# The last store of an attention-score kernel, issued as three transfers

## The chip, the cores and the metric

The kernel runs on one core of one Trainium2 chip. The metric is the device time of one execution in microseconds (us), on that one core. Beside it there is a profile of one execution, whose span runs from its first to its last instruction and is a little shorter than the time.

## The reference

For 64 heads (batch 8, heads 8) of 512 positions and 64 features, all products of a query with a key, scaled:

```python
def setup_inputs():
    batch, heads, seq, dim = 8, 8, 512, 64
    return {"q": np.random.randn(batch, heads, seq, dim).astype(np.float32),
            "k": np.random.randn(batch, heads, seq, dim).astype(np.float32)}

def reference(q, k):
    scale = 1.0 / np.sqrt(q.shape[-1])
    return (np.einsum('bhqd,bhkd->bhqk', q, k) * scale).astype(np.float32)
```

The inputs are 16.8 MB together and the output is 67.1 MB in float32, so most of what the core moves is output.

## The kernel before

The work is cut into 16 tiles (`CHUNKS * UNITS`, four each), numbered by `g`. One tile is the scores of four heads: 128 partitions x 2 x 4096 float32, 4 MB. Here `P` is 128, `RO` is 8 and `S` is 512. A partition of a tile holds two runs (`x`) of `RO * S` = 4096 numbers, 16 KB each, and each run is contiguous in the output as well. Three buffers in SBUF, `bigs`, take turns; the loaded inputs pass through them too.

```python
    store_sems = [nc.alloc_semaphore(f"store{n}") for n in range(3)]
    ...
    out_r = out.rearrange("(v b) (t x h) (u i) k -> (v b t) (h u) x (i k)", b=2, x=2, h=2, i=RO)

    bigs = [nc.alloc_sbuf_tensor(f"big{n}", [P, 2, RO, S], f32)[:] for n in range(3)]
    ...
    def store_buffer(g):
        return bigs[(0, 2, 1)[g % 3]]
```

The inputs are loaded, cast to bfloat16 by GpSimd, transposed and multiplied by TensorE. ScalarE and VectorE move the products from PSUM to the tile's buffer, 128 x 1024 numbers at a time, and scale them on the way:

```python
        for g in range(CHUNKS * UNITS):
            o = store_buffer(g)
            for p in range(parity, PAIRS, 2):
                ...
                scaled(o[:, x, i:i + 2, :], pss[p % 3]).then_inc(
                    sem[f"free{p % 3}"] if p < PAIRS - 2 else drained, 1)
```

(`drained` is `out_act` for ScalarE and `out_dve` for VectorE.) SyncE issues one store for each tile once both engines have finished it, and at the end waits for all stores. The increment of `next` lets TensorE go on to a further tile:

```python
    for g in range(CHUNKS * UNITS):
        nc.sync.wait_ge(sem["out_act"], g + 1)
        nc.sync.wait_ge(sem["out_dve"], g + 1).then_inc(sem["next"], 1)
        nc.sync.dma_start(out=out_r[g], in_=store_buffer(g).rearrange("p x i k -> p x (i k)")
                          ).then_inc(store_sems[g % 3], 16)
    for n in range(3):
        nc.sync.wait_ge(store_sems[n], 16 * len(range(n, 4 * UNITS, 3)))
```

A store counts as done when its semaphore has gone up by 16; in the trace these arrive as 16 single landings[...]. GpSimd waits for the store two tiles back before it lets a buffer be filled again:

```python
    for g in range(2, CHUNKS * UNITS - 1):
        ...
        nc.gpsimd.wait_ge(store_sems[(g - 2) % 3], 16 * ((g - 2) // 3 + 1)
                          ).then_inc(sem["room"], 1)
```

Of the kernel before, what the change touches and what calls it, by code (L numbers as in the profile page):

```python
# [5 lines left out]
def kernel(  # L6
# [5 lines left out]
    nc = tc.nc  # L12
    B, H, S, D = q.shape
    scale = 1.0 / (D ** 0.5)
    P = 128
    UNITS = B // 2
# [4 lines left out]
    RO = 8  # L21
# [6 lines left out]
    CHUNKS = 4  # L28
# [10 lines left out]
    sem = {name: nc.alloc_semaphore(name) for name in names}  # L39
    load_sems = [nc.alloc_semaphore(f"load{n}") for n in range(2 * UNITS)]  # L40
    store_sems = [nc.alloc_semaphore(f"store{n}") for n in range(3)]

    q_r = q.rearrange("(v b) g (m j) d -> v (b g m) (j d)", b=2, j=R)
    k_r = k.rearrange("(v b) g (m j) d -> v (b g m) (j d)", b=2, j=R)
    out_r = out.rearrange("(v b) (t x h) (u i) k -> (v b t) (h u) x (i k)", b=2, x=2, h=2, i=RO)
# [26 lines left out]
    def xf(v):  # L72
        return bigs[(0, 1, 2, 1)[v]].rearrange("p x i k -> p (x i k)").rearrange(
            "p (x s c) -> p x s c", x=2, s=2)

    def store_buffer(g):
        return bigs[(0, 2, 1)[g % 3]]

    def load(v, x):
        nc.sync.dma_start(out=xf(v)[:, x],  # L80
                          in_=(k_r, q_r)[x][v].rearrange("p (s c) -> p s c", s=2)
                          ).then_inc(load_sems[2 * v + x], 16)
# [9 lines left out]
    for x in range(2):  # L92
        nc.sync.wait_ge(sem["cast"], x + 1)
        load(UNITS - 1, x)
    for g in range(CHUNKS * UNITS):
        nc.sync.wait_ge(sem["out_act"], g + 1)
        nc.sync.wait_ge(sem["out_dve"], g + 1).then_inc(sem["next"], 1)
        nc.sync.dma_start(out=out_r[g], in_=store_buffer(g).rearrange("p x i k -> p x (i k)")
                          ).then_inc(store_sems[g % 3], 16)
    for n in range(3):  # L100
        nc.sync.wait_ge(store_sems[n], 16 * len(range(n, 4 * UNITS, 3)))


    nc.gpsimd.memset(identity, 0.0).then_inc(sem["ident"], 1)
# [10 lines left out]
    def cast(v, x, s, j0, j1, dst):  # L115
        src = xf(v)[:, x, s]
        if x == 0:
            src = src.rearrange("p (j e d) -> p j e d", e=2, d=D)[:, j0:j1]
            dst = dst[:, :, s].rearrange("p j d e -> p j e d")
        else:  # L120
            src = src.rearrange("p (j e i d) -> p j e i d", e=2, i=RO, d=D)
            dst = dst[:, :, s].rearrange("p (i j) d e -> p j e i d", i=RO)
        return nc.gpsimd.tensor_copy(out=dst, in_=src)  # L123

    for v in range(UNITS):
        for x in range(2):
# [4 lines left out]
            if v == 1 and x == 0:  # L131
# [3 lines left out]
                last = cast(v, x, 1, 0, W, xs)  # L135
                last.then_inc(sem["ready"], 1)
            else:
                for s in range(2):
                    last = cast(v, x, s, 0, JP, xb[:, w0:w0 + JP])
# [140 lines left out]
```

## Time and profile before

| what | value |
|---|---|
| time, median of 3 executions (lowest to highest) | 203.05 us (202.89 to 203.07) |
| span of the profiled execution | 201.3 us |
| TensorE busy | 100.6 us, 50% |
| VectorE busy | 106.2 us, 53% |
| ScalarE busy | 86.8 us, 43% |
| GpSimd busy | 58.4 us, 29% |
| moved by DMA | 83.91 MB, mean 417 GB/s |
| read from and written to HBM | 16.78 MB and 67.11 MB |
| stores | 16, of 4096 KB each, median 19.7 us from issue to landing |
| loads | 8, of 2048 KB each, median 15.3 us (k) and 17.8 us (q) |

How to read it: the busy times say how long each engine worked and not whether it set the pace. The time from issue to landing of a transfer includes its wait behind those issued earlier. The page also has a row that gives the mean busy share of the core's 16 DMA engines in 40 slices of the span, in tenths, and under it the rate in GB/s. For finer questions the trace can be asked for any stretch of the span: busy time of each engine, share and rate of the DMA engines there (a packet counts for the stretch in which it starts).

### The profile page before, as it was taken

What the parts mean: (1) busy time and instruction counts of PE and PEld (TensorE: products, weight loads), DVE (VectorE), ACT (ScalarE), POOL (GpSimd) and SP (SyncE); (2) the same over time, 40 slices, a digit from 0 to 9 for tenths busy, and PEclk for the clock granted to TensorE, in tenths of its full rate; (3) what the DMA queues carried; (4) which work ended last, traced back from release to release, by engine and by line L of the source; (5) the groups of instructions that cost most, each with busy time, mean ns of one, the idle gap of its engine ahead of it and who ended that gap; (6) DMA issues with size and microseconds to landing.
All of it is one profiled execution on the core that took longest, in us unless ns stands there. A gap on an engine that the chain in (4) does not pass through costs nothing. (4 is left out here: it accounts for less than half of the span.)

```text
span 201.3 us, 1617 instructions
## 1 busy us (share of the span) xinstructions
PE 100.6 (50%) x368; PEld 50.0 (25%) x384; DVE 106.2 (53%) x98; ACT 86.8 (43%) x98; POOL 58.4 (29%) x34
## 2 busy tenths in 40 slices
PE   0037492375667637566665775477536464730000
PEld 0036350141334314232431333143202121200000
DVE  0665556076847696575769375927653636350000
ACT  0204576264645657374656355635434444440000
POOL 0399999999303030303030303030000000000000
PEclk9999969579957999888899589957996969696555
DMA  6999999999999999999999999999999999999993
GB/s 202 423 420 446 433 423 430 433 413 433 420 426 446 423 426 436 433 423 426 446 423 430 436 433 420 430 443 423 430 430 439 423 423 433 433 425 423 426 436 150
DMA packets 5507, 83.91 MB, mean 417 GB/s; under 512 B 384, under 2 KB 384, under 8 KB 384
## 3 DMA queue, kind: packets, MB, share of 16 engines
q1 hardware_dynamic: 5504, 83.89, 98.1%
q14 instruction: 3, 0.02, 0.0%
HBM read 16.78 MB, written 67.11 MB: 417 GB/s over the span
## 5 line engine op out<-in xcount | busy, mean ns | idle before, releaser
L173 PE MATMUL ps<-kT,qz 128*128 x240 | 79.7, 452 | 61.7 <-PEq L162 60.1
L247 DVE TENSOR_SCALAR big<-ps 128x1024 f32<-128x1024 f32 x64 | 77.0, 1222 | 51.5 <-PE ps L173 51.1
L244 ACT ACTIVATE big<-ps 128x1024 f32<-128x1024 f32 x64 | 64.9, 1023 | 69.4 <-PE ps L173 66.8
L173 PEld LDWEIGHTS ps<-kT,qz 128*128 x256 | 27.7, 108 | 106.8 <-issue 100.9
L112 POOL COPY xs<-xb 128x2048 bf16<-128x2048 bf16 x10 | 18.9, 1893 | 67.2 <-DMA out_dram<-big 67.0
L123 POOL CAST xb<-big 128x2048 bf16<-128x2048 f32 (+1 forms) x16 | 36.3, 2321 | 3.5 <-DMA big<-in_k_dram 2.8
L158 PE MATMUL tp<-identity,xs 128*128 128x128 f32 x96 | 17.8, 347 | 1.1 <-PEq L162 1.1
L158 PEld LDWEIGHTS tp<-identity,xs 128*128 128x128 f32 x96 | 16.1, 187 | 5.8 <-issue 5.2
L216 DVE COPY kT<-tp 64x512 f32<-64x512 f32 x14 | 9.7, 694 | 6.3 <-PE tp L158 5.8
L216 ACT COPY kT<-tp 64x512 f32<-64x512 f32 x14 | 8.1, 577 | 11.4 <-PE tp L158 11.2
L216 DVE COPY qz<-tp 64x512 f32<-64x512 f32 x12 | 8.3, 694 | 6.3 <-PE tp L158 6.1
L221 DVE MEMSET qz<- 128x4096 uint32 x2 | 6.9, 3472 | 6.8 <-PEq L89 6.0
L216 ACT COPY qz<-tp 64x512 f32<-64x512 f32 x12 | 7.5, 621 | 3.0 <-PE tp L158 2.8
L158 PE MATMUL tp<-identity,xb 128*128 128x128 f32 x8 | 1.9, 424 | 13.5 <-PEq L162 13.5
L158 PE MATMUL ps<-identity,xb 128*128 128x128 f32 x24 | 5.6, 422 | 1.3 <-PEq L162 1.3
L158 PEld LDWEIGHTS ps<-identity,xb 128*128 128x128 f32 x24 | 5.0, 228 | 1.6 <-issue 1.6
L158 PEld LDWEIGHTS tp<-identity,xb 128*128 128x128 f32 x8 | 1.6, 223 | 13.5 <-issue 13.5
L216 DVE COPY qz<-ps 64x512 f32<-64x512 f32 x4 | 2.8, 694 | 2.1 <-PE ps L158 2.1
L216 ACT COPY qz<-ps 64x512 f32<-64x512 f32 x4 | 2.6, 641 | 2.5 <-PE ps L158 2.4
L216 ACT ACT_TABLE_LOAD x1 | 1.3, 1283 | 5.0 <-PEq L89 5.0
L123 POOL CAST xs<-big 128x1024 bf16<-128x1024 f32 x2 | 2.7, 1337 | 0.2 <-DMA big<-in_k_dram 0.2
L112 ACT COPY xs<-xb 128x2048 bf16<-128x2048 bf16 x1 | 1.9, 1891 | 0.0
(8 smaller groups left out, 3.4 us busy)
## 6 DMA issues: line engine op xcount, KB each, us to landing
out_dram<-big SPq DMA_DIRECT2D x16, 4096.0 KB, 19.7
big<-in_k_dram SPq DMA_DIRECT2D x4, 2048.0 KB, 15.3
big<-in_q_dram SPq DMA_DIRECT2D x4, 2048.0 KB, 17.8
```

Source lines behind the costliest of these rows:

```text
L112: copy(out=xs.rearrange("p w s d e -> p (w s d e)"), in_=xb[:, w0:w0 + W].rearrange("p w s d e -> p (w s d e)")).then_inc(sem["ready"], 1)
L123: return nc.gpsimd.tensor_copy(out=dst, in_=src)
L158: ins = pe.transpose(out=dst[:, w], identity=identity, in_=src[:, w])
L173: ins = pe.matmul(out=ps[:, w, :], lhsT=qz[:, bass.ds(n2 + x, 1), i + w].rearrange("p n c -> p (n c)"), rhs=keys[:, bass.ds(n2 + x, 1)].re ...
L216: copy(out=dst, in_=src[:, h]).then_inc(sem["moved"], 1)
L221: engine.memset(qz[:, v * N:(v + 1) * N], 0.0).then_inc(sem["zeroed"], 1)
L244: lambda o, ps: nc.scalar.mul(out=o, in_=ps, mul=scale),
L247: lambda o, ps: nc.vector.tensor_scalar(out=o, in0=ps, scalar1=scale, scalar2=None, op0=mult),
```

## The change

The stores of the first 15 tiles stay. The last tile's store becomes three transfers, each with a semaphore of its own. `edge` is 3072 numbers, so the first transfer takes the first 12 KB of each run of all 128 partitions. The second takes the remaining 4 KB of each run of partitions 0 to 119, and the third the same of partitions 120 to 127. By the change's description the first runs over 16 DMA engines, the second over 15 and the third over 8. It is for the end of the kernel: it deals the last tile's bytes unequally over the DMA engines, with fewer of them for one engine.

```diff
+    part_sems = [nc.alloc_semaphore(f"part{n}") for n in range(3)]
 ...
+    edge = 3 * RO * S // 4
+    parts = [(slice(0, P), slice(0, edge)), (slice(0, P - 8), slice(edge, RO * S)),
+             (slice(P - 8, P), slice(edge, RO * S))]
+    last = CHUNKS * UNITS - 1
     for g in range(CHUNKS * UNITS):
         nc.sync.wait_ge(sem["out_act"], g + 1)
         nc.sync.wait_ge(sem["out_dve"], g + 1).then_inc(sem["next"], 1)
-        nc.sync.dma_start(out=out_r[g], in_=store_buffer(g).rearrange("p x i k -> p x (i k)")
-                          ).then_inc(store_sems[g % 3], 16)
+        src = store_buffer(g).rearrange("p x i k -> p x (i k)")
+        if g < last:
+            nc.sync.dma_start(out=out_r[g], in_=src).then_inc(store_sems[g % 3], 16)
+        else:
+            for n, (rows, cols) in enumerate(parts):
+                nc.sync.dma_start(out=out_r[g][rows, :, cols], in_=src[rows, :, cols]
+                                  ).then_inc(part_sems[n], 16)
     for n in range(3):
-        nc.sync.wait_ge(store_sems[n], 16 * len(range(n, 4 * UNITS, 3)))
+        nc.sync.wait_ge(store_sems[n], 16 * len(range(n, last, 3)))
+    for n in range(3):
+        nc.sync.wait_ge(part_sems[n], 16)
```

## The prediction, made before the changed kernel ran

> **What bounds the kernel now.** I read the page's second and third parts first. The span is 201.3 us, and in all but its first and last slices the DMA engines are at nine tenths:
>
> ```profile
> DMA  6999999999999999999999999999999999999993
> GB/s 202 423 420 446 433 423 430 433 413 433 420 426 446 423 426 436 433 423 426 446 423 430 436 433 420 430 443 423 430 430 439 423 423 433 433 425 423 426 436 150
> ...
> q1 hardware_dynamic: 5504, 83.89, 98.1%
> ```
>
> One queue on 16 engines moves 83.89 MB and is busy for 98.1% of the span, so the kernel is bound by its transfers and no arithmetic matters. The reader is to see the exception: the last slice, digit 3 at 150 GB/s. Then the waits of the queue that issues the transfers, and the end of its timeline:
>
> ```profile
> SPq L97 <- DVE big L247: 143.5, 16, 13.6
> SPq L101 <- DMA out_dram<-big: 21.4, 2, 19.4
> ```
>
> ```profile
> 179.51 0.37 SPq L98 DMA_DIRECT2D out_dram<-big  x1
> ```
>
> The last of the 16 stores is issued at 179.51 and the rest of the span is its landing: 201.3 - 179.5 = 21.8 us. A store of 4 MB at 430 GB/s is 9.75 us; the other 12 us are the store ahead of it in the queue and the drain. Nothing computes after VectorE's eviction at 178.19, so the end is set by DMA alone. I cut the last 5 us into stretches of 0.6 us (columns: stretch, length, the engines' busy times with counts, granted clock, mean busy share of the 16 DMA engines, GB/s):
>
> ```profile
> 197.00:197.60 0.60, 0.00 (x0) 0.00 (x0) 0.00 (x0) 0.00 (x0) 0.00 (x0) 0.50 1.03 437
> 197.60:198.20 0.60, 0.00 (x0) 0.00 (x0) 0.00 (x0) 0.00 (x0) 0.00 (x0) 0.50 0.39 164
> 198.20:198.80 0.60, 0.00 (x0) 0.00 (x0) 0.00 (x0) 0.00 (x0) 0.00 (x0) 0.50 0.07 27
> 198.80:199.40 0.60, 0.00 (x0) 0.00 (x0) 0.00 (x0) 0.00 (x0) 0.00 (x0) 0.50 0.06 27
> 199.40:200.00 0.60, 0.00 (x0) 0.00 (x0) 0.00 (x0) 0.00 (x0) 0.00 (x0) 0.50 0.06 27
> 200.00:200.60 0.60, 0.00 (x0) 0.00 (x0) 0.00 (x0) 0.00 (x0) 0.00 (x0) 0.50 0.06 27
> 200.60:201.30 0.70, 0.00 (x0) 0.00 (x0) 0.00 (x0) 0.00 (x0) 0.00 (x0) 0.50 0.00 0
> ```
>
> This is the finding. A share of 0.06 is one engine of 16 (1/16 = 0.0625); 27 GB/s for 0.6 us is 16 KB, one packet, which is one run of the store. From 198.2 on four such packets start one after the other on a single engine while fifteen have nothing left: 4 x 16 KB = 64 KB in 2.4 us. The trace's record of single landings says the same: of the last store's 16 landings, 14 fall within 0.5 us, the fifteenth 0.3 us later, and the sixteenth 2.16 us after that, at the span's end. The lag is no accident of the last store: with tiles numbered from 0, the last landing is behind the fifteenth by 0.5 us for store 0, 0.2 for store 3, 1.0 for store 6, 1.7 for store 9, and 2.1 to 2.3 for stores 11 to 15. One engine is slower and never catches up, because each store gives each engine 256 KB.
>
> [...] The trace shows one slow engine (and a fifteenth landing 0.3 us late), but not its number.[...]
>
> **The change part by part.** All of it is in the last store's 4 MB; 15 stores, loads and compute stay. The instruction order differs only in the issuing queue: 15 whole stores and three partial ones.
>
> *Removed.* [...] It keeps 8 partitions x 2 runs x 12 KB = 192 KB of 256 KB, so 64 KB fewer: 4 packets of 0.607 us (start to start) = 2.43 us. If it is the slow one, its last data moves from 200.86 (last packet's end) to 198.43.
>
> *Added to others.* The second transfer is 120 x 2 x 4 KB = 960 KB over 15 engines: 64 KB each, as before. The third is 8 x 2 x 4 KB = 64 KB over 8 engines: 8 KB each[...], at 27 GB/s 0.30 us. They were done between 198.0 and 198.7, so they would be done between 198.3 and 199.0.
>
> *Smaller packets and more transfers.* An engine that had 16 packets of 16 KB has 16 of 12 KB and 16 of 4 KB, and two more semaphore writes. The semaphore packets take 9 ns each in the trace. Packets of 4 KB don't occur in it; I allow 0.1 us in all, a guess.
>
> *Issue.* Two more issues of 0.37 us, at about 179.9 and 180.3; the queue still has the store before to move until about 188, so they are hidden. Three more waits at the end have a length of tens of ns (17 ns for the shorter of the two recorded on that line); after landing nothing else is added.
>
> Sum where everything goes as meant: the end of data goes from 200.86 to the later of 198.5[...] and 198.7 to 199.1 (the rest), so 1.8 to 2.2 us less: about 201.1 us of 203.05.
>
> [...]
>
> **The rivals.**
> 1. *The second transfer collides on ports.* [...] 960 KB at about 217 GB/s is 4.8 us instead of 2.4. [...] Against: the change's cut of 64 KB fits the lag closely, as if sized by someone who saw it work.
> 2. *The slow engine isn't the one relieved.* [...] nothing is saved (203.1 to 203.3); [...] it gets 8 KB more, and 203.4 to 204.2. For it: the trace doesn't number engines. [...]
> 3. *The lag belongs to the profiled execution.* In the last 20 us, with compute over, the lag stays at 2.1 to 2.2 us and doesn't grow: all packets then take about 611 ns, while the slow ones before had 634 to 644. So the slow engine is disturbed by something that goes with compute, and that might be the recording itself. Then only the cost of the pieces stays: 203.1 to 204.2. Against: the executions that were timed take 203.05 us, no less than the profiled one's 202.65, where a missing 2 us of tail should show.
> 4. *The pieces land one row after the other in a worse order*[...]. I give it little.
>
> **Range and chances.** As meant without port trouble, 201.1 us: 0.30. With the third transfer slowed, 201.5 to 202.1: 0.25. Rival 1, near 203.9: 0.19. Rivals 2 and 3, 203.1 to 204.2: 0.22. Rival 4: 0.04. The middle of this lies near 202; I put the one figure at 201.8 us, between the two good cases and the rest, and the range from 200.8 to 204.1. The gain can't pass the whole lone tail, 2.4 us or 1.2%, so faster by over 2% (below 199.0) is next to impossible: 0.01. Slower by over 2% needs 4 us (rival 4 or two rivals at once): 0.04. The rest, 0.95, is within 2%.
>
> **What would show it.** Right: in stretches of 0.6 us at the end, the share falls from 1.0 to 0 within about 1.5 us and no run of lines with 0.06 and 27 GB/s is left. [...] Rival 1: for 4 to 5 us before the end a rate near 217 GB/s with the share still near 1, since packets of 4 KB would take about 300 ns instead of about 155. Rival 2: the same 2.4 us of single packets at the end as before. Rival 3: the profiled tail shrinks but the timed executions don't. Wrong altogether: a time below 200.8 us, which would mean that more than the tail had moved, or one above 204.1 us.

## The result, and the profile after

| | before | changed |
|---|---|---|
| time, median (lowest to highest) | 203.05 us (202.89 to 203.07) | 203.34 us (203.22 to 203.65) |
| ratio of the times, 95% interval | 1 | 1.0019 (1.0001 to 1.0036) |
| the same in a later measurement, with 15 executions of the changed kernel | 1 | 1.0021 (1.0013 to 1.0029) |
| span of the profiled execution | 201.3 us | 202.0 us |

The change made the kernel slower by some 0.4 us, where 1.25 us faster was predicted. The page of the changed kernel shows no difference but in the last slices:

```profile
DMA  6999999999999999999999999999999999999995
GB/s 198 428 435 432 425 438 422 428 393 438 425 428 441 425 425 441 422 425 451 422 422 448 422 425 441 425 428 425 444 428 422 444 425 422 441 423 428 419 378 163
...
q1 hardware_dynamic: 5783, 83.89, 98.4%
```

The bytes are the same 83.89 MB. The last slice rose from 3 to 5 tenths busy, but at nearly the same rate, 163 GB/s instead of 150, and the slice before it fell to 378: the engines are busy for longer over the same bytes. The issuing queue's waits, and the instructions that wrote the output (least, median and greatest ns of one, first and last start in us):

```profile
SPq L104 <- DVE big L261: 143.9, 16, 12.9
SPq L115 <- DMA out_dram<-big: 18.6, 3, 16.0
```

```profile
L107 SPq DMA_DIRECT2D out_dram<-big x15: 372/372/402, 34.7 to 169.7; - x15
L110 SPq DMA_DIRECT2D out_dram<-big x3: 372/1277/1404, 180.1 to 182.0; - x3
```

The waits for computing are what they were. In order of time the three issues took 0.37 us (16 engines), 1.40 us (15) and 1.28 us (8), where 0.37 us each was expected, but all three were issued by 183.3, long before an engine needed them. So the loss is in the drain. The end of the span in stretches of 0.6 us (last two columns: mean busy share of the 16 DMA engines, GB/s):

```profile
195.50:196.10 0.60, 0.00 (x0) 0.00 (x0) 0.00 (x0) 0.00 (x0) 0.00 (x0) 0.50 0.75 273
196.10:196.70 0.60, 0.00 (x0) 0.00 (x0) 0.00 (x0) 0.00 (x0) 0.00 (x0) 0.50 1.05 246
196.70:197.30 0.60, 0.00 (x0) 0.00 (x0) 0.00 (x0) 0.00 (x0) 0.00 (x0) 0.50 0.90 205
197.30:197.90 0.60, 0.00 (x0) 0.00 (x0) 0.00 (x0) 0.00 (x0) 0.00 (x0) 0.50 0.83 205
197.90:198.50 0.60, 0.00 (x0) 0.00 (x0) 0.00 (x0) 0.00 (x0) 0.00 (x0) 0.50 0.87 300
...
200.30:200.90 0.60, 0.00 (x0) 0.00 (x0) 0.00 (x0) 0.00 (x0) 0.00 (x0) 0.50 0.14 55
200.90:201.50 0.60, 0.00 (x0) 0.00 (x0) 0.00 (x0) 0.00 (x0) 0.00 (x0) 0.50 0.07 27
```

Two things stand here. From 196 to 198 the share is near 1 and the rate is 205 to 246 GB/s: packets of 4 KB take nearly twice their time (half of those that start there take 293 ns or more; with the pieces alone, below, the mean is 162). And there is again a stretch of one engine alone (0.07, 27 GB/s), only shorter, because the others now end later.

The record of single landings tells more. I read a landing as the end of one engine's part: the last whole store before has 16 landings, and the last of them comes at 201.29, 0.43 us after the end of the last lone packet. Each transfer has its own semaphore, so for each one its last landing can be read, and the one before it (us of the span). The numbers of engines are as described: near the end the three transfers have 16, 15 and 8 landings. The trace doesn't number the engines.

| | store of tile 14, last | first transfer: 15th, last | second: last but one, last | third: last but one, last |
|---|---|---|---|---|
| changed kernel | 191.90 | 198.42, 199.19 | 201.05, 201.66 | 201.37, 201.96 |
| the same, other execution | 191.69 | 198.35, 198.98 | 200.92, 201.45 | 201.24, 201.75 |

Read the last landings across as one engine's work: 7.29 us for its 192 KB of the first transfer, 2.47 us for 64 KB, 0.30 us for 8 KB, in both executions to 0.01 us. That fits one engine working without a stop through all three transfers. By this reading the slow engine takes part in the second transfer, from which the change was to keep it out, and even in the third. In the kernel before, the slow engine took 9.68 us for its 256 KB (191.61 to 201.29), now 7.29 + 2.47 + 0.30 = 10.06. The experiments tested this reading.

### The profile page after: what moved, and what is told of

Same layout as the page of the kernel before. It is cut to its first block, busy times and chain, and to the rows that moved or that the text cites. A ratio compares the mean times of both kernels' runs of the same rounds, so it can differ in the third digit from the quotient of the medians.

```text
span 202.0 us, 1636 instructions
## 1 busy us (share of the span) xinstructions
PE 104.4 (52%) x384; PEld 50.6 (25%) x384; DVE 106.3 (53%) x98; ACT 87.2 (43%) x98; POOL 58.5 (29%) x34
## 3 DMA queue, kind: packets, MB, share of 16 engines
q1 hardware_dynamic: 5783, 83.89, 98.4%
## 5 line engine op out<-in xcount | busy, mean ns | idle before, releaser
L187 PE MATMUL ps<-kT,qz 128*128 x256 | 83.8, 464 | 58.8 <-PEq L176 58.6
```

Of the source, the lines that this page charges most:

```text
L187: ins = pe.matmul(out=ps[:, w, :], lhsT=qz[:, bass.ds(n2 + x, 1), i + w].rearrange("p n c -> p (n c)"), rhs=keys[:, bass.ds(n2 + x, 1)].re ...
```

## The experiments

In each kernel only `edge` and `parts` of the changed kernel are edited, with as many semaphores and waits as there are parts. Ratios are to the kernel before, on the same chip, with 95% intervals. The theories: *wrong engine* (the slow engine isn't the one relieved), *ports* (engines that read certain partitions slow one another on a shared path, and that costs the gain in the second and third transfer; an assumption, since the trace names no path and shows only packets with their sizes and times), *pieces* (smaller packets and more transfers cost it).

**Pieces alone**

```diff
-    parts = [(slice(0, P), slice(0, edge)), (slice(0, P - 8), slice(edge, RO * S)),
-             (slice(P - 8, P), slice(edge, RO * S))]
+    parts = [(slice(0, P), slice(0, edge)), (slice(0, P), slice(edge, RO * S))]
```

> The last store in two pieces, 12 KB and 4 KB of each run, both of all 128 partitions over 16 engines: no engine is relieved[...], only the packets of 4 KB and one more transfer are kept. If sharing of SBUF ports eats the gain (ports theory)[...]: the time of the kernel before within 0.2 us (203.0 to 203.25), a lone engine of 2 to 2.4 us at the end, and nearly all 4 KB packets at 159 ns. If pieces and small packets cost the time (pieces theory), some 1.5 us of slow 4 KB packets show here too: 203.8 us or more.

Measured: 202.98 us, ratio 1.0001 (0.9992 to 1.0011). The tail of the kernel before is there:

```profile
197.60:198.20 0.60, 0.00 (x0) 0.00 (x0) 0.00 (x0) 0.00 (x0) 0.00 (x0) 0.50 0.97 389
198.20:198.80 0.60, 0.00 (x0) 0.00 (x0) 0.00 (x0) 0.00 (x0) 0.00 (x0) 0.50 0.24 96
198.80:199.40 0.60, 0.00 (x0) 0.00 (x0) 0.00 (x0) 0.00 (x0) 0.00 (x0) 0.50 0.07 27
199.40:200.00 0.60, 0.00 (x0) 0.00 (x0) 0.00 (x0) 0.00 (x0) 0.00 (x0) 0.50 0.07 27
200.00:200.60 0.60, 0.00 (x0) 0.00 (x0) 0.00 (x0) 0.00 (x0) 0.00 (x0) 0.50 0.07 27
```

The 4 KB packets take 162 ns on average (171 at most), against 213 (701 at most) in the changed kernel. The slow engine needs 7.30 + 2.45 = 9.75 us, 0.07 more than before: that is the whole price of the pieces. The pieces theory is out.

**Without the third transfer**

```diff
-    parts = [(slice(0, P), slice(0, edge)), (slice(0, P - 8), slice(edge, RO * S)),
-             (slice(P - 8, P), slice(edge, RO * S))]
+    parts = [(slice(0, P), slice(0, edge)), (slice(0, P - 8), slice(edge, RO * S))]
```

> The changed kernel without its third transfer (the last 4 KB of each run of partitions 120 to 127 is not stored: 64 KB left out). Ports theory: [...] leaving them out gives about 0.7 to 1.2 us: 202.2 to 202.6 us against 203.3; the second transfer's collisions stay. Pieces theory: 8 KB fewer[...], 0.3 us: 203.0 us.

Measured: 202.99 us, ratio 1.0008 (1.0000 to 1.0016). The 64 KB left out are worth about 0.3 us and not 0.7 to 1.2. The slow engine takes 7.28 + 2.47 = 9.75 us, what it took with the pieces alone. The 203.0 us that the pieces theory expected is met, since it rested on the same 8 KB for each of eight engines; what it said of small packets is out all the same. So the second transfer doesn't relieve the slow engine at all, and of the changed kernel's 0.38 us (10.06 - 9.68) 0.30 is the third transfer's 8 KB on the slow engine. A path shared by eight readers isn't needed to explain it.

**Partitions 32 to 91 against 0 to 59.** The second transfer takes half of each run, of 60 partitions over 15 engines by the landings; the rest isn't stored. Only which 60 differs:

```diff
-    edge = 3 * RO * S // 4
+    edge = RO * S // 2
+    parts = [(slice(0, P), slice(0, edge)), (slice(32, 92), slice(edge, RO * S))]
     # and, in the second kernel of the pair, slice(0, 60) for slice(32, 92)
```

> The last store as 8 KB of each run of all 128 partitions, then the other 8 KB of partitions 32 to 91 alone, 60 rows over 15 engines, four rows each; the rest isn't stored (1.06 MB left out). [...] Ports theory: second transfer at full rate, 64 KB per engine in 2.4 us, time about 198.8 us, 8 KB packets at about 310 ns. Pieces theory: the same time as for partitions 0 to 59.

> As the run with partitions 32 to 91, with partitions 0 to 59 in their place: the same bytes, packets, pieces and engines[...]. Ports theory: second transfer at half rate, 4.8 us, so 2.1 us more than with partitions 32 to 91: about 200.9 us, 8 KB packets at about 600 ns. Pieces theory: the same as with partitions 32 to 91 within 0.2 us.

Measured: 200.56 us with partitions 32 to 91 (ratio 0.9885, 0.9869 to 0.9902) and 200.84 us with 0 to 59 (0.9896, 0.9880 to 0.9913). By the times alone both theories missed: the pair differs by 0.28 us and not by 2.1, and the first is 1.8 us later than expected. The second is at the 200.9 us of the ports theory by luck, since another engine ended it, as the landings below show. The traces tell why. Partitions 32 to 91:

```profile
194.00:194.60 0.60, 0.00 (x0) 0.00 (x0) 0.00 (x0) 0.00 (x0) 0.00 (x0) 0.50 0.94 396
194.60:195.20 0.60, 0.00 (x0) 0.00 (x0) 0.00 (x0) 0.00 (x0) 0.00 (x0) 0.50 0.98 410
195.20:195.80 0.60, 0.00 (x0) 0.00 (x0) 0.00 (x0) 0.00 (x0) 0.00 (x0) 0.50 0.72 300
195.80:196.40 0.60, 0.00 (x0) 0.00 (x0) 0.00 (x0) 0.00 (x0) 0.00 (x0) 0.50 0.14 55
196.40:197.00 0.60, 0.00 (x0) 0.00 (x0) 0.00 (x0) 0.00 (x0) 0.00 (x0) 0.50 0.06 27
197.00:197.60 0.60, 0.00 (x0) 0.00 (x0) 0.00 (x0) 0.00 (x0) 0.00 (x0) 0.50 0.06 27
```

Partitions 0 to 59:

```profile
194.00:194.60 0.60, 0.00 (x0) 0.00 (x0) 0.00 (x0) 0.00 (x0) 0.00 (x0) 0.50 0.91 218
194.60:195.20 0.60, 0.00 (x0) 0.00 (x0) 0.00 (x0) 0.00 (x0) 0.00 (x0) 0.50 0.99 232
195.20:195.80 0.60, 0.00 (x0) 0.00 (x0) 0.00 (x0) 0.00 (x0) 0.00 (x0) 0.50 0.98 232
195.80:196.40 0.60, 0.00 (x0) 0.00 (x0) 0.00 (x0) 0.00 (x0) 0.00 (x0) 0.50 0.92 205
196.40:197.00 0.60, 0.00 (x0) 0.00 (x0) 0.00 (x0) 0.00 (x0) 0.00 (x0) 0.50 0.91 205
```

The same bytes and sizes, over 15 engines each, move at about 400 GB/s in one and about 220 in the other, and the 8 KB packets take 312 and 628 ns in the median (about 310 and 600 expected). Fourteen engines land between 195.98 and 196.59 with partitions 32 to 91. With 0 to 59 thirteen land between 198.31 and 198.96 and one at 196.26, as early as with 32 to 91. So the choice of partitions alone halves the rate, as expected. Engines that slow one another in pairs, with one of the 15 left over, would fit it, but which engines meet, and where, isn't shown. And in both runs the fifteenth landing is later still (199.09 and 199.46). In the first it comes 2.44 us after the last landing of the first transfer. That is the slow engine, at the full rate of its 64 KB and inside a transfer over 15 engines. So *wrong engine* sets the end, and the halved rate only uses up time beside it.

**Which engine?**

```diff
+    edge = 15 * RO * S // 16
+    parts = [(slice(0, P), slice(0, edge))]
+    row = 0
+    for k in range(8, 0, -1):
+        parts.append((slice(row, row + k), slice(edge, RO * S)))
+        row += k
```

> Which engine is slow? The last store as 15 KB of each run of all 128 partitions, then eight small transfers of the last 1 KB for 8, 7, 6, ... 1 partitions (0 to 7, 8 to 14, and so on; partitions 36 to 127 keep their last 1 KB unstored), so over 8, 7, 6, ... 1 engines. A transfer that the slow engine takes part in has one landing some 2.3 us behind its others. [...] a late landing in the transfer over 8 engines and in none over 7 or fewer. [...]

Measured in a single execution, the last two landings of each transfer in us:

```
engines      8               7               6               5               4
landings  198.88, 201.25  199.06, 201.43  199.23, 201.62  199.42, 201.81  199.40, 199.61
```

A landing is 2.4 us late with 8, 7, 6 and 5 engines and not in the four transfers after them. (The last of these, of one partition, had two landings where one was expected.) So seven engines don't leave the slow engine out, as I had expected, and neither do six or five; four do. I call it the fifth, on the reading that a smaller transfer takes some of the engines of a larger one: it fits these landings, but the trace gives the engines no numbers. The transfers over 15 engines don't spare it either: in the changed kernel and in both runs with 60 partitions I read the fifteenth landing as its. The ladder ran once, on one chip. On another chip the slow engine took part in the changed kernel's transfer over eight engines (last landings 201.45 and 201.75, 0.30 us apart), and the transfers over four, with 16 KB less for it, below, left it out (9.09 us of work, not 9.68).

**Four partitions beside the slow engine's tail**

```diff
+    edge = RO * S // 2
+    parts = [(slice(0, P), slice(0, edge)), (slice(24, 28), slice(edge, RO * S))]
     # and slice(28, 32), and slice(16, 20), in the other two
```

> The last store as 8 KB of each run of all 128 partitions, then the other 8 KB of partitions 24 to 27 only, over four engines (the rest isn't stored, 2.03 MB left out). Those four rows [...] take 64 KB / 27 GB/s = 2.4 us, beside the slow engine's tail of 2.4 us. Both theories of what holds the tail (the slow engine alone; the port that it reads) expect the same: the first transfer's last landing near 196.7 us of the span, the second's near 196.1 to 196.7, time about 198.2 us.

> As the run with partitions 24 to 27, with partitions 28 to 31[...]. If the port holds the tail, the two streams share 27 GB/s: 64 KB more go through the port after the same start and the last landing comes 2.4 us later, near 199 us of the span, time about 200.6 us; so moving these bytes to other engines would gain nothing. If the slow engine alone holds it, the same as with partitions 24 to 27, about 198.2 us.

> [...] So the run with partitions 24 to 27 again, now with 16 to 19 (the rest isn't stored). If the port that the slow engine reads holds the tail, the 64 KB of the second transfer and the slow engine's last 64 KB share one port: the last landing comes 2.4 us later than with 24 to 27, near 199.1 us of the span, time about 200.5 us. If only the engine is the limit, nothing is delayed: 198.1 us.

Measured: 198.12 us (0.9766, 0.9748 to 0.9783), 198.22 us (0.9770, 0.9752 to 0.9788) and 198.14 us (0.9767, 0.9750 to 0.9783). In all three the four engines bring 64 KB in 2.3 to 3.0 us, together at about one engine's rate (64 KB in 2.4 us) or less. Which partitions the slow engine reads in its tail is not shown; that its path is the one of 28 to 31, or after the ladder the one of 16 to 19, was assumed. If the second holds, the run with 16 to 19 speaks against the theory that a shared path holds the tail: the slow engine landed at 196.61, as in the other two (196.68, 196.71). The four newcomers waited instead, and the last of them landed at 196.64, 0.67 us later than with 24 to 27. Partitions 24 to 27, then 16 to 19:

```profile
194.00:195.00 1.00, 0.00 (x0) 0.00 (x0) 0.00 (x0) 0.00 (x0) 0.00 (x0) 0.50 0.22 49
195.00:196.00 1.00, 0.00 (x0) 0.00 (x0) 0.00 (x0) 0.00 (x0) 0.00 (x0) 0.50 0.08 33
```

```profile
194.00:195.00 1.00, 0.00 (x0) 0.00 (x0) 0.00 (x0) 0.00 (x0) 0.00 (x0) 0.50 0.08 33
195.00:196.00 1.00, 0.00 (x0) 0.00 (x0) 0.00 (x0) 0.00 (x0) 0.00 (x0) 0.50 0.22 49
```

With 16 to 19 the newcomers start almost nothing from 194 to 195: four of their eight packets take 1.53 to 1.82 us, where the longest with 24 to 27 takes 1.18, while the slow engine's stay at 309 ns each. The two streams together moved some 128 KB from 193.5 to 196.6, 42 GB/s and more than the 27 GB/s of one engine, or of the four newcomers together. So the slow engine's tail isn't the full load of a path that it shares with these partitions, or it shares none with them; which of the two stays open.

**Other cuts of the third transfer.** Seven partitions and one, then four and four:

```diff
 ...
+             (slice(P - 8, P - 1), slice(edge, RO * S)), (slice(P - 1, P), slice(edge, RO * S))]
     # and slice(P - 8, P - 4) with slice(P - 4, P)
```

> The changed kernel with its third transfer cut in two: 7 partitions over 7 engines and 1 partition over one, all bytes stored. [...] it no longer gets the last 8 KB, and 0.30 us of the changed kernel's loss goes: 203.0 to 203.1 us, ratio to the kernel before about 1.000. [...] the time stays at about 203.3 us (1.0019) or rises by some tenths.

> The changed kernel with its third transfer cut into two of 4 partitions each[...] (all bytes stored). [...] it no longer gets 8 KB at the very end and the 0.30 us between the second and the third transfer's last landing goes: 203.0 to 203.1 us, ratio about 1.0005. If the loss came from elsewhere, it stays at 203.3 us or more.

Measured: 203.52 us, ratio 1.0031 (1.0021 to 1.0041), and 203.40 us, ratio 1.0029 (1.0020 to 1.0037). Seven engines don't leave the slow engine out: last landings 201.57 and 201.87, 0.30 us apart as before. (The one partition again had two landings.) With four and four the slow engine is free of the third transfer, as expected (its last landing is the second transfer's, at 201.64, and 7.28 + 2.48 = 9.76 us in all), but the time didn't fall: the expected 1.0005 lies outside the interval. That profile has one of the shorter executions (span 201.8); they range from 201.6 to 202.6. What ended last in the longer ones isn't shown. A candidate, not tested: in the changed kernel a second engine is 2 us late in the first transfer (198.42, against 196.43 for the fifteenth with pieces alone), so more than one engine is near the end.

**Where the collisions are.** One transfer reads 1 KB of each run of every fourth partition in turn. If it meets the slow engine on a path, its packets there should be slow:

```diff
+    edge = 15 * RO * S // 16
+    parts = [(slice(0, P), slice(0, edge)), (slice(0, 121, 4), slice(edge, RO * S))]
```

> Which port does the slow engine read in its tail? After 15 KB of each run of all 128 partitions, one transfer of 31 partitions (0, 4, 8 ... 120)[...], reads 1 KB of each run in turn (the rest of the last KB isn't stored). [...] the 1 KB packets of partitions 16 and 48 take twice as long as the others (about 90 ns against 46 ns) or longer. If another pair of partitions is slow, that is its port. If none is slow, the tail takes up no port's full rate.

Measured in a single execution: all 54 packets that started from 199.3 on took 46 ns, while the slow engine still had large packets until 200.85: from there on it slowed the scan at no partition. (The rate was 46 GB/s from 199.2 to 199.8 and 49 from 199.8 to 200.4, which fits two engines: the slow one's 27 and the 22 of 1 KB in 46 ns.) The slow ones were all before 199.3: partitions 0 (311 and 395 ns), 4 (332) and 12 (295). In that time four other engines had a 15 KB packet of 1.28 to 1.52 us in place of 0.57. So in this execution both lost in the stretch in which one engine entered its next transfer while others finished the last one. Partitions 16 and 48, for which I had assumed a path shared with the slow engine, showed nothing.

**Relieving the right engine.** Transfers over four engines, which by the ladder and by four and four leave the slow engine out, take the end of each run:

```diff
+    edge = 31 * RO * S // 32
+    parts = [(slice(0, P), slice(0, edge)), (slice(0, P - 4), slice(edge, RO * S)),
+             (slice(P - 4, P), slice(edge, RO * S))]
```

```diff
+    edge = 15 * RO * S // 16     # and 59 * RO * S // 64
+    parts = [(slice(0, P), slice(0, edge)), (slice(0, 116), slice(edge, RO * S))]
+    parts += [(slice(116 + j, P, 3), slice(edge, RO * S)) for j in range(3)]
```

> An attempt to relieve the engine that is slow: the last 0.5 KB of each run of all partitions goes[...] (124 partitions in one transfer, 4 in another), the first 15.5 KB over all 16. [...] If only the engine is the limit[...]: 202.6 us of 202.9, ratio 0.9985. If the port that it reads is the limit, its bytes go through that port in any case: no gain, ratio 1.000 or somewhat above.

> All bytes stored. The last 1 KB of each run of all partitions goes[...]; the first 15 KB over all 16. The slow engine has 16 KB less, 0.61 us. If the slow engine alone holds the tail (the scan's reading: its tail slowed no port)[...]: about 202.3 us, ratio 0.997. If its partitions' port holds the tail: 202.8 to 202.9 us, ratio 1.000.

> The same with 1.25 KB: the slow engine has 20 KB less, 0.76 us[...]. Engine theory: 202.1 to 202.3 us, ratio 0.996 to 0.997, near the best of this kind. Port theory: 1.000 or above.

> The change as it is, once more, beside the two that relieve the engine found slow, for a ratio from more executions of one chip: 1.002, and again a last landing of the third transfer 0.3 us after the second's last.

Measured: 202.77 us, ratio 0.9997 (0.9989 to 1.0006) with 8 KB less for the slow engine; 204.79 us, 1.0085 (1.0070 to 1.0099) with 16 KB less; 205.00 us, 1.0113 (1.0096 to 1.0130) with 20 KB less; the change again 203.18 us, 1.0021. The slow engine does end earlier by what is taken off it: from its landing of tile 14's store it needs 9.40, 9.09 and 8.93 us, against 9.68 (expected 9.38, 9.07 and 8.92). So the engine theory is right for that engine, and the expected time is wrong all the same, because the four that take over are slow. With 16 KB less:

```profile
198.00:199.00 1.00, 0.00 (x0) 0.00 (x0) 0.00 (x0) 0.00 (x0) 0.00 (x0) 0.50 0.20 55
199.00:200.00 1.00, 0.00 (x0) 0.00 (x0) 0.00 (x0) 0.00 (x0) 0.00 (x0) 0.50 0.31 76
200.00:201.00 1.00, 0.00 (x0) 0.00 (x0) 0.00 (x0) 0.00 (x0) 0.00 (x0) 0.50 0.23 54
201.00:202.00 1.00, 0.00 (x0) 0.00 (x0) 0.00 (x0) 0.00 (x0) 0.00 (x0) 0.50 0.26 86
202.00:203.00 1.00, 0.00 (x0) 0.00 (x0) 0.00 (x0) 0.00 (x0) 0.00 (x0) 0.50 0.13 45
```

From 198 to 201, for most of which large packets are still under way (the last ends at 200.35), the rate is 54 to 76 GB/s; 24 of 121 recorded 1 KB packets take 100 to 518 ns. From 201 to 202 the rate is 86 GB/s at a share of 0.26, four engines' worth of 16, and from 201 on nearly all take 46 ns. From its first to its last small packet the work of the four engines took 5.4 us (197.7 to 203.2) and not the 2.7 us on which the expected time rested, though the last issue was done by 196.5, and the last landing is theirs, at 203.75 (the slow engine's: 200.79). The smallest shift ends about even: the four at 201.08, the slow engine at 201.24. None of these versions is measurably faster than the kernel before.

## Why the prediction was wrong, point by point

- *The kernel is bound by DMA, and its end by one engine alone for 2.4 us*: right, and the stretches show it in every run that stores evenly.
- *Removed: 64 KB from one engine, so the slow engine ends at 198.43*: this is the step that failed. The prediction said "if it is the slow one"; it isn't. The slow engine lost no byte and gained 8 KB, its work grew from 9.68 to 10.06 us, and its last packet ended at 201.54. I gave the condition too much weight because the cut fitted the lag; but the fit of a size says nothing on whom it is taken from, and no trace of before showed which engine would be relieved.
- *Added: 8 KB, 0.30 us, on each of eight engines*: right to the hundredth, but on the slow engine. Rival 2 said this with 203.4 to 204.2 us; 203.34 and 203.18 lie just under its lower edge. The stated range of 200.8 to 204.1 us holds the measured time because the rivals were in it; the figure of 201.8 us stood on the cases that relieve the slow engine.
- *Pieces, 0.1 us, a guess*: 0.07 us.
- *Issue, 0.37 us each*: 1.40 and 1.28 us, hidden as said.
- *The third transfer slowed, 201.5 to 202.1 us in all*: an estimate that no trace of before showed, and not seen as such. The engines that come late to it needed 0.30 to 0.32 us, by the last two landings; that the others had passed by then is the likely reason.
- *Rival 1, collisions in the second transfer at half rate*: right in the rate (205 to 246 GB/s in the changed kernel, 217 expected, half of the 434 that whole stores moved; the 4.8 us in the prediction are twice 2.4 us, and 960 KB at 217 GB/s are 4.5). It cost the other engines about 2.1 us (the last but one landing of the second transfer is 201.05, against 198.91 with pieces alone), nearly all beside the slow engine's tail. Had the slow engine been relieved as meant, the others' last landing, 201.37, would have left at most 0.4 us of the predicted gain in that profile, an estimate from 201.79 with pieces alone.
- *Rival 3, a lag that belongs to the recording*: no run tested it. What makes the engine slow during compute stays open.
- *Rival 4, a much slower order*: did not happen.

So the gain went twice: it was aimed at another engine, and most of what it freed would have gone to the second transfer's halved rate. The loss of 0.38 us on the slow engine in the two profiled executions is 0.30 for the third transfer and 0.08 for the pieces. The times don't confirm this split as the whole cost: leaving the third transfer out brought the ratio from 1.0019 to 1.0008, but keeping it off the slow engine, in two transfers of four partitions, left it at 1.0029, and what ended those executions stays open.

## What to carry to other kernels

A lone tail at one engine's rate shows that an engine is late and not which; before bytes are taken off it, find it with a few transfers over 8, 7, 6, 5 and 4 engines (and over more, if none of them is late), each with a semaphore of its own, and look for the late landing. Pieces of 4 KB of 128 partitions moved at 389 to 437 GB/s (195.8 to 198.2 with pieces alone), the same of 120 at 205 to 246; pieces of 8 KB of partitions 32 to 91 at about 400, of 0 to 59 at about 220. So when work is moved between DMA engines by cutting partitions, the rate of the cut has to be measured, and not only its bytes counted. When the intervals between the last landings of successive transfers repeat to the hundredth and fit the bytes of one engine, they are likely one engine's work, and here that was a sharper tool than the total time.

## What was not expected of the hardware

- Issuing the transfers over 15 and 8 engines took 1.40 and 1.28 us, one over 16 engines 0.37 us. In the run with 16 KB less for the slow engine, the transfer of 116 partitions over four engines took 10.3 us to issue.
- Four engines reading four neighbouring partitions brought 64 KB in 2.3 us (partitions 24 to 27), about what one engine took for it (2.45 us).
- Small and large packets were both slow where they met: 1 KB packets of 46 ns took up to 518 ns while 15 KB packets were under way, and in the scan four 15 KB packets took 1.28 to 1.52 us instead of 0.57.
